# Order of the 512- and 256-column products in the half blocks of a two-layer streaming encoder

## The chip, the cores and the metric

The kernel runs on one core of one Trainium2 chip. The time is the device time of one execution in microseconds (us). The profile is of another execution of the same program; its engines are PE (TensorE matmuls), PEld (TensorE weight loads), DVE (VectorE), ACT (ScalarE), POOL (GpSimd) and SP (which issues most DMAs).

## The reference

Two layers on 256 tokens of width 2048, all float32. Layer 0 is a gated DeltaNet mixer, layer 1 a chunked softmax attention; around the mixers stand four large projections, which are the matrix products spoken of here.

```python
def gated_deltanet(h, w_in, conv_w, a_log, dt_bias, out_norm_w, w_out):
    proj = h @ w_in          # 2048 -> 4*2048 + 32
    qkv = silu(causal_depthwise_conv(proj[..., :3*2048], conv_w))
    ...                      # L2 norms, decay, delta rule in chunks of 64, scan
    return (rms_norm(o, out_norm_w) * silu(z)) @ w_out

def chunk_band_attention(h, w_in, q_norm_w, k_norm_w, rel_bias, w_out):
    proj = h @ w_in          # 2048 -> 4*2048
    ...                      # 9-chunk key band, bias, softmax, gate silu(z)
    return o @ w_out

for i in range(2):
    h = h + mixer[i](rms_norm(h, norm_w[i]))
```

## The kernel before

All weights are read once from memory, 320 pieces of 512 KB called chunks, in the order of a list `plan`. I number them from 0 in that order. `fetch()` runs up to three chunks ahead (`LOOK`): SP loads the chunk into `wt` (4 buffers), ACT rounds it to `whi` (L195, "hi"), and DVE computes the rest `wlo = wt - whi` (L196, "lo"). `whi` and `wlo` have 3 buffers each, so the hi of a chunk can be made when TensorE has used the hi of the chunk three before it, and likewise the lo.

The activations stand in `xb[:, kt, a, :]` as hi (a = 0) and lo (a = 1), 256 tokens each. A product of weights and activations is hi\*hi + hi\*lo + lo\*hi. In a *half* block (152 of the 320 chunks) a chunk has 256 output features and four k-tiles, and `features2` makes the sum with two kinds of product: a **long** one of 512 columns (hi weights on hi and lo activations side by side, L238) and a **short** one of 256 columns (lo weights on the hi activations, L241). There are eight of each in a chunk (two features' halves `s` times four k-tiles `j`). `GROUP = 2` cuts the chunk into two groups of two k-tiles: four long, four short, four long, four short. Each product loads its own 128x128 weights. A half block is four chunks into one PSUM tile `psp` (2 buffers); when it is done, ACT copies one part of it (`ev`, L304) and DVE adds the other (L305), and the tile is free for the block after the next. The other blocks are *wide* (`features`, L228 to L231, all of 256 columns) and *tokens* (L247 to L249, all of 512 columns).

Work that is not a projection (convolutions L497 and L499, norms, the q/k products L556, their scaling L560, squares L568, the copies L606 and transposition L616 of the inversion) stands in background generators; `step()` runs a piece of them after each group. What comes out is then ordered on each engine by a scheduler when the program is built; each engine runs its list strictly in that order. `pre` lets a chunk wait, in the program's text, until its activations have been written.

Of the kernel before, what the change touches and what calls it, by code (L numbers as in the profile page):

```python
# [14 lines left out]
P = 128  # L15
# [3 lines left out]
KT = D // P  # L19
# [4 lines left out]
NWARM = 12  # L24
TIE0 = 4
TIE = 2
GROUP = 2


C_CONV = 0  # L30
# [10 lines left out]
def tile_hybrid_trunk(  # L41
# [12 lines left out]
    act, dve, pool, pe = nc.scalar, nc.vector, nc.gpsimd, nc.tensor  # L54
# [9 lines left out]
    def ps_small():  # L64
        return pss.tile([P, 512], F32, name="pss", tag="pss")
# [19 lines left out]
    ps = ps_small()  # L85
# [124 lines left out]
    def step(n=1):  # L210

        while now:
            now.pop(0)()
        for _ in range(n):
            lanes = (bgq, bg2) if turn[0] else (bg2, bgq)
            turn[0] ^= 1
            for lane in lanes:
                if advance(lane):
                    break
# [10 lines left out]
        pe.matmul(ps, lhsT=hi[:, j, fs], rhs=xb[:, kt, 1, :], start=False, stop=False, skip_group_check=True)  # L230
        pe.matmul(ps, lhsT=lo[:, j, fs], rhs=xb[:, kt, 0, :], start=False, stop=(kt == KT - 1), skip_group_check=True)  # L231

    def features2(ps, hi, lo, js, ks, xb):


        both = [(s, j) for j in js for s in range(2)]
        for s, j in both:
            pe.matmul(ps[:, s], lhsT=hi[:, j, s * P:(s + 1) * P], rhs=xb[:, ks[j], :, :], start=(ks[j] == 0), stop=False,  # L238
                      skip_group_check=True)
        for s, j in both:  # L240
            pe.matmul(ps[:, s, 0, :], lhsT=lo[:, j, s * P:(s + 1) * P], rhs=xb[:, ks[j], 0, :], start=False,  # L241
                      stop=(ks[j] == KT - 1), skip_group_check=True)

    def tokens(ps, t, j, kt, hi, lo, xb):
        ts_ = slice(t * P, (t + 1) * P)
# [7 lines left out]
    def chunk(kind, ps, xb, rate=1, pre=None):  # L253
        i = state["use"]
        state["use"] += 1
        while state["next"] < min(i + 1 + LOOK, len(plan)):
            fetch()
        hi, lo = fetched.pop(i)
        kc = KC * 512 // plan[i][3]
        ks = [plan[i][2] * kc + j for j in range(kc)]  # L260
        f, ns = KINDS[kind]
        if i == len(plan) - 1:

            out_pre(ps)
            for s in range(ns):
                fs = slice(s * P, (s + 1) * P)
                for j, kt in enumerate(ks):
                    for w, a in ((hi, 0), (hi, 1), (lo, 0)):
                        pe.matmul(ps[:, s, 0, :], lhsT=w[:, j, fs], rhs=xb[:, kt, a, :], start=False,
                                  stop=(kt == KT - 1 and w is lo), skip_group_check=True)  # L270
                out_part(s, ps)
            return
        if kind == "half":
            for j in range(0, kc, GROUP):
                js = range(j, j + GROUP)
                if pre is not None:
                    for jj in js:
                        pre(ks[jj])
                features2(ps, hi, lo, js, ks, xb)
                step(rate)  # L280
            return
        for j, kt in enumerate(ks):
            if pre is not None:
                pre(kt)
            for s in range(ns):
                f(ps[:, s], s, j, kt, hi, lo, xb)
            step(rate)
# [6 lines left out]
    def block(kind, xb, rate=1, pre=None):  # L294
        ps = acc(kind)
        for _ in range(CPH if kind == "half" else CPB):
            chunk(kind, ps, xb, rate, pre)
        return ps
# [10 lines left out]
    def pair(xb, rate=1, pre=None):  # L309

        evs = []
        for _ in range(2):
            joined(block("half", xb, rate, pre), evs)
        return evs
# [17 lines left out]
    def split_tiles():  # L332
        return slot("xb", 32, F32R).rearrange("p (k a t) -> p k a t", k=KT, a=2)
# [32 lines left out]
    xb = split_tiles()  # L366
# [460 lines left out]
    for gi in range(4):  # L827
        ps = pair(xb, 2) if gi else block("features", xb, pre=x_split)
# [11 lines left out]
    for gi in range(3):  # L840
        ps = block("tokens", xb, 2 if gi else 1)
# [5 lines left out]
    for gi in range(4):  # L847
        ps = pair(xb)
# [63 lines left out]
    for n in (CUT, CPB - CUT):  # L912
        for j in range(2):
            if n != CUT and j == 0:
                drain()
            for _ in range(n):
                chunk("features", pa[j], gmem["b"], 2, ready(gmem))
            if n != CUT:
                a_done(j, pa[j], 4 * j, 4 * j + 4)
# [20 lines left out]
    xb = hmem["x"]  # L940
    pb, evs = [acc("half") for _ in range(2)], []
    for n in (CUTH, CPH - CUTH):
        for j in range(2):
            if n != CUTH and j == 0:
                drain()
            for _ in range(n):
                chunk("half", pb[j], xb, 2, ready(hmem))
            if n != CUTH:
                joined(pb[j], evs)
# [127 lines left out]
    last = {}  # L1077

    def out_pre(ps):
        last["o"] = o = wk("cv")  # L1080
        dve.tensor_tensor(out=o[:, 0:2, :], in0=ps[:, :, 1, :], in1=h_r[:, 14:16, :], op=ALU.add)

    def out_part(s, ps):
        o = last["o"][:, s, :]
        dve.tensor_tensor(out=o, in0=ps[:, s, 0, :], in1=o, op=ALU.add)
        nc.sync.dma_start(out=ov[:, 14 + s, :], in_=o)
# [69 lines left out]
```

## Time and profile before

| | us |
|---|---|
| median of the runs | 1024.39 |
| the profiled execution | 1024.26 |
| its span (first to last instruction) | 1022.4 |
| PE busy | 1007.9 (99%) |
| PEld busy | 881.1 (86%) |
| DVE busy | 694.8 (68%) |
| ACT busy | 520.2 (51%) |

The span is what the profiler saw between the first and the last instruction; 1.9 us of the execution lie around it. Matmuls overlap in the pipeline, so the time of one is read from the start of one to the start of the next, not from its own duration.

### The profile page before, as it was taken

To read this page: it belongs to the slowest core of one execution; us is meant where nothing else is said; L and a number is where in the kernel's file an instruction comes from. 1 tells how busy PE (TensorE), PEld (TensorE's weight loads), DVE (VectorE), ACT (ScalarE), POOL (GpSimd) and SP (SyncE) were. 2 spreads that over 40 slices of the span, in tenths; PEclk is the share of its full clock that TensorE was granted. 3 is DMA by queue.
4 is the path that set the end of the run, shared out by engine and by line. 5 is a ranking of instruction groups with operands and counts; after the bars stand their busy time and mean duration, and the time that the engine had idled before them with its cause. 6 is when DMAs were issued, how large, how long until landed. Compare 5 with 4: busy or idle time off the path is not lost.

```text
span 1022.4 us, 15569 instructions
## 1 busy us (share of the span) xinstructions
PE 1007.9 (99%) x6094; PEld 881.1 (86%) x6094; DVE 694.8 (68%) x1111; ACT 520.2 (51%) x720; POOL 76.3 (7%) x91
## 2 busy tenths in 40 slices
PE   8999999999999999999999999999999999999998
PEld 7988788888788989899988888888888888889987
DVE  6699879998799587755766555444456666656553
ACT  7465756453646555544654444444445555555442
POOL 1004000112000000001000000000011010101000
PEclk9999999999999999999999999999999999999999
DMA  8655566555576355545856766666665555554572
GB/s 292 177 147 144 162 175 180 143 164 158 157 199 165 105 145 145 158 151 157 255 186 183 228 207 205 190 194 195 188 188 176 148 178 151 167 163 146 174 227 72
DMA packets 133736, 177.55 MB, mean 174 GB/s; under 512 B 7584, under 2 KB 89632, under 8 KB 133664
## 3 DMA queue, kind: packets, MB, share of 16 engines
q1 hardware_dynamic: 132512, 172.38, 57.1%
q0 software_dynamic: 1152, 4.19, 1.2%
q8 instruction: 47, 0.77, 0.3%
q14 instruction: 25, 0.20, 0.1%
HBM read 174.46 MB, written 2.10 MB: 173 GB/s over the span
## 4 chain that ended last, share of the span: by engine, by line
PE 95%; DVE 2%; ACT 1%; DMA 1%; issue 1%; SPq 0%; DVEq 0%; ACTq 0%
PE psp L238 27%; PE psp L241 14%; PE psp L248 11%; PE psp L249 11%; PE psp L247 11%; PE psp L231 4%; PE psp L228 4%; PE psp L230 4%; PE pss L556 2%; PE pss L753 1%; PE pss L992 1%; PE pss L1011 1%; PE pss L1047 1%; DMA wt<-in_a_w_in_dram 1%; DVE wlo L196 1%; PE pss L1037 1%
## 5 line engine op out<-in xcount | busy, mean ns | idle before, releaser
L196 DVE TENSOR_TENSOR wlo<-wt,whi 128x1024 fp32r<-128x1024 f32 (+1 forms) x321 | 392.9, 1226 | 247.2 <-ACT whi L195 238.8
L195 ACT CAST whi<-wt 128x1024 fp32r<-128x1024 f32 (+1 forms) x321 | 336.7, 1050 | 410.9 <-PE psp L238 164.0
L238 PE MATMUL psp<-xb,whi 128*128 128x512 f32 x960 | 265.7, 396 | 3.6 <-DVE ev L305 2.0
L248 PE MATMUL psp<-wlo,xb 128*128 128x512 f32 x512 | 201.1, 393 | 1.6 <-DVE wlo L196 1.6
L249 PE MATMUL psp<-whi,xb 128*128 128x512 f32 x512 | 201.5, 393 | 0.0
L247 PE MATMUL psp<-whi,xb 128*128 128x512 f32 x512 | 200.0, 391 | 0.0
L238 PEld LDWEIGHTS psp<-xb,whi 128*128 128x128 f32 x960 | 165.0, 190 | 25.9 <-DVE ev L305 2.2
L241 PEld LDWEIGHTS psp<-xb,wlo 128*128 128x128 f32 x960 | 148.4, 189 | 20.1
L241 PE MATMUL psp<-xb,wlo 128*128 128x256 f32 x960 | 157.6, 283 | 0.0
L248 PEld LDWEIGHTS psp<-wlo,xb 128*128 128x128 f32 x512 | 96.1, 188 | 21.7 <-DVE wlo L196 2.0
L247 PEld LDWEIGHTS psp<-whi,xb 128*128 128x128 f32 x512 | 96.2, 188 | 20.1 <-ACT whi L195 0.3
L249 PEld LDWEIGHTS psp<-whi,xb 128*128 128x128 f32 x512 | 96.2, 188 | 19.1
L228 PE MATMUL psp<-g,whi 128*128 128x256 f32 x256 | 73.4, 287 | 0.0
L230 PE MATMUL psp<-g,whi 128*128 128x256 f32 x256 | 73.3, 287 | 0.0
L231 PE MATMUL psp<-g,wlo 128*128 128x256 f32 x256 | 72.7, 284 | 0.0
L238 PE MATMUL psp<-g,whi 128*128 128x512 f32 x248 | 67.7, 394 | 0.0
L499 DVE SCALAR_TENSOR_TENSOR cv<-raw,sm,cv 128x254 f32<-128x254 f32 (+2 forms) x144 | 61.8, 474 | 0.1
L230 PEld LDWEIGHTS psp<-g,whi 128*128 128x128 f32 x256 | 49.1, 192 | 0.2
L228 PEld LDWEIGHTS psp<-g,whi 128*128 128x128 f32 x256 | 49.1, 192 | 0.1
L231 PEld LDWEIGHTS psp<-g,wlo 128*128 128x128 f32 x256 | 49.1, 192 | 0.1
L238 PEld LDWEIGHTS psp<-g,whi 128*128 128x128 f32 x248 | 42.4, 189 | 5.7
L241 PEld LDWEIGHTS psp<-g,wlo 128*128 128x128 f32 x248 | 38.1, 189 | 5.3
(239 smaller groups left out, 980.1 us busy)
## 6 DMA issues: line engine op xcount, KB each, us to landing
wt<-in_b_w_in_dram SPq DMA_DIRECT2D x128, 512.0 KB, 3.7
wt<-in_a_w_in_dram SPq DMA_DIRECT2D x127, 512.0 KB, 3.9
wt<-in_a_w_out_dram SPq DMA_DIRECT2D x32, 512.0 KB, 4.5
wt<-in_b_w_out_dram SPq DMA_DIRECT2D x32, 512.0 KB, 4.0
g<-in_xT_dram SPq DMA_DIRECT2D x8, 256.0 KB, 4.5
dl<-in_xT_dram POOLq DMA_DIRECT2D x4, 512.0 KB, 5.4
dl<-in_relb_dram POOLq DMA_DIRECT2D x4, 512.0 KB, 5.2
out_dram<-cv SPq DMA_DIRECT2D x2, 512.0 KB, 4.2
```

The source lines that it names most:

```text
L195: act.copy(out=hi[:, js], in_=wt[:, js])
L196: dve.tensor_tensor(out=lo[:, js], in0=wt[:, js], in1=hi[:, js].bitcast(F32), op=ALU.subtract)
L228: pe.matmul(ps, lhsT=hi[:, j, fs], rhs=xb[:, kt, 0, :], start=(kt == 0 and s % 2 == 0), stop=False, skip_group_check=True)
L230: pe.matmul(ps, lhsT=hi[:, j, fs], rhs=xb[:, kt, 1, :], start=False, stop=False, skip_group_check=True)
L231: pe.matmul(ps, lhsT=lo[:, j, fs], rhs=xb[:, kt, 0, :], start=False, stop=(kt == KT - 1), skip_group_check=True)
L238: pe.matmul(ps[:, s], lhsT=hi[:, j, s * P:(s + 1) * P], rhs=xb[:, ks[j], :, :], start=(ks[j] == 0), stop=False, skip_group_check=True)
L241: pe.matmul(ps[:, s, 0, :], lhsT=lo[:, j, s * P:(s + 1) * P], rhs=xb[:, ks[j], 0, :], start=False, stop=(ks[j] == KT - 1), skip_group_chec ...
L247: pe.matmul(ps, lhsT=xh, rhs=hi[:, j, :], start=(kt == 0), stop=False)
L248: pe.matmul(ps, lhsT=xh, rhs=lo[:, j, :], start=False, stop=False)
L249: pe.matmul(ps, lhsT=xl, rhs=hi[:, j, :], start=False, stop=(kt == KT - 1))
L499: dve.scalar_tensor_tensor(out=cv[:, i, s:], in0=raw[:, i, :T - s], scalar=conv_w(i0 + i, 3 - s), in1=cv[:, i, s:], op0=ALU.mult, op1=ALU.add)
L556: pe.matmul(dst, lhsT=kq[:, a, i, c:c + P], rhs=rhs, start=(n == 0), stop=(n == 2))
```

## The change

The groups are gone. In a half chunk all eight long products now stand together and all eight short ones together, and the order of the two alternates from chunk to chunk: the first and third chunk of a block begin with the long ones, the second and fourth with the short ones. So the short products at the end of one chunk meet the short ones of the next, and runs of sixteen alike come about. Inside a run the k-tiles now follow each other within one feature half (`s` outside, `j` inside; before `j` was outside). `features2` is a generator and yields after each run, so there are still two `step()` calls for a chunk; `pre` is called once, for the chunk's last k-tile. The last chunk of the program has its own code and is as it was.

```diff
--- before.py
+++ after.py
@@ -24,7 +24,6 @@
 NWARM = 12
 TIE0 = 4
 TIE = 2
-GROUP = 2
 
 
 C_CONV = 0
@@ -230,16 +229,22 @@
         pe.matmul(ps, lhsT=hi[:, j, fs], rhs=xb[:, kt, 1, :], start=False, stop=False, skip_group_check=True)
         pe.matmul(ps, lhsT=lo[:, j, fs], rhs=xb[:, kt, 0, :], start=False, stop=(kt == KT - 1), skip_group_check=True)
 
-    def features2(ps, hi, lo, js, ks, xb):
-
-
-        both = [(s, j) for j in js for s in range(2)]
-        for s, j in both:
-            pe.matmul(ps[:, s], lhsT=hi[:, j, s * P:(s + 1) * P], rhs=xb[:, ks[j], :, :], start=(ks[j] == 0), stop=False,
-                      skip_group_check=True)
-        for s, j in both:
-            pe.matmul(ps[:, s, 0, :], lhsT=lo[:, j, s * P:(s + 1) * P], rhs=xb[:, ks[j], 0, :], start=False,
-                      stop=(ks[j] == KT - 1), skip_group_check=True)
+    def features2(ps, hi, lo, ks, xb):
+
+
+        both = [(s, j) for s in range(2) for j in range(len(ks))]
+        turns = (ks[0] // len(ks)) % 2
+        for n, long in enumerate((not turns, turns)):
+            for s, j in both:
+                w = (hi if long else lo)[:, j, s * P:(s + 1) * P]
+                last = n == 1 and ks[j] == KT - 1
+                if long:
+                    pe.matmul(ps[:, s], lhsT=w, rhs=xb[:, ks[j], :, :], start=(ks[j] == 0), stop=last,
+                              skip_group_check=True)
+                else:
+                    pe.matmul(ps[:, s, 0, :], lhsT=w, rhs=xb[:, ks[j], 0, :], start=False, stop=last,
+                              skip_group_check=True)
+            yield
 
     def tokens(ps, t, j, kt, hi, lo, xb):
         ts_ = slice(t * P, (t + 1) * P)
@@ -271,12 +276,9 @@
                 out_part(s, ps)
             return
         if kind == "half":
-            for j in range(0, kc, GROUP):
-                js = range(j, j + GROUP)
-                if pre is not None:
-                    for jj in js:
-                        pre(ks[jj])
-                features2(ps, hi, lo, js, ks, xb)
+            if pre is not None:
+                pre(ks[-1])
+            for _ in features2(ps, hi, lo, ks, xb):
                 step(rate)
             return
         for j, kt in enumerate(ks):
```

The program has the same instructions on every engine as before. In their order, longs that follow each other make 98 runs in place of 314 and shorts 109 in place of 322 (57 runs of sixteen longs, 17 of eight; 55 of sixteen shorts, 14 of eight; the others are broken by background products). The scheduler has also moved background work.

The first place is on PE, chunks 31, 32 and 33 (`whi_1209`, `whi_1234`, `whi_1256` and their lo; `psp_1207` and `psp_1299` are the PSUM tiles of two blocks). Before:

```order
L238 MATMUL psp_1207<-xb_108,whi_1209 128x512 x4
L241 MATMUL psp_1207<-xb_108,wlo_1210 128x256 x4
L238 MATMUL psp_1207<-xb_108,whi_1209 128x512 x4
L241 MATMUL psp_1207<-xb_108,wlo_1210 128x256 x4
L238 MATMUL psp_1299<-xb_108,whi_1234 128x512 x4
L241 MATMUL psp_1299<-xb_108,wlo_1235 128x256 x4
L238 MATMUL psp_1299<-xb_108,whi_1234 128x512 x4
L241 MATMUL psp_1299<-xb_108,wlo_1235 128x256 x4
L238 MATMUL psp_1299<-xb_108,whi_1256 128x512 x4
L241 MATMUL psp_1299<-xb_108,wlo_1257 128x256 x4
L238 MATMUL psp_1299<-xb_108,whi_1256 128x512 x4
L241 MATMUL psp_1299<-xb_108,wlo_1257 128x256 x4
```

and now:

```order
L245 MATMUL psp_1207<-xb_108,wlo_1210 128x256 x8
L242 MATMUL psp_1207<-xb_108,whi_1209 128x512 x8
L242 MATMUL psp_1299<-xb_108,whi_1234 128x512 x8
L245 MATMUL psp_1299<-xb_108,wlo_1235 128x256 x8
L245 MATMUL psp_1299<-xb_108,wlo_1257 128x256 x8
L242 MATMUL psp_1299<-xb_108,whi_1256 128x512 x8
```

Chunk 31 begins with its shorts, its longs meet those of chunk 32, and the shorts of 32 meet those of 33.

The second place is on DVE, at the addition that frees the PSUM tile `psp_1080` for chunk 32 (`ev_1222`, L305 before, L307 now). Before:

```order
L196 TENSOR_TENSOR wlo_1210<-wt_1208,whi_1209 128x1024
L527 TENSOR_REDUCE ssq_113<-raw_952 128x8
L196 TENSOR_TENSOR wlo_1235<-wt_1233,whi_1234 128x1024
L320 TENSOR_TENSOR raw_1098<-ev_1003,rB_561 128x512
L320 TENSOR_TENSOR raw_1098<-ev_1095,rB_561 128x512
L196 TENSOR_TENSOR wlo_1257<-wt_1255,whi_1256 128x1024
L499 SCALAR_TENSOR_TENSOR cv_1101<-raw_1098,sm_76,cv_1101 128x255 x2
L305 TENSOR_TENSOR ev_1222<-psp_1080,ev_1222 128x512
L499 SCALAR_TENSOR_TENSOR cv_1101<-raw_1098,sm_76,cv_1101 128x255
```

and now:

```order
L195 TENSOR_TENSOR wlo_1235<-wt_1233,whi_1234 128x1024
L529 TENSOR_REDUCE ssq_113<-raw_952 128x8
L195 TENSOR_TENSOR wlo_1257<-wt_1255,whi_1256 128x1024
L322 TENSOR_TENSOR raw_1098<-ev_1003,rB_561 128x512
L322 TENSOR_TENSOR raw_1098<-ev_1095,rB_561 128x512
L195 TENSOR_TENSOR wlo_1279<-wt_1277,whi_1278 128x1024
L501 SCALAR_TENSOR_TENSOR cv_1101<-raw_1098,sm_76,cv_1101 128x255 x2
L307 TENSOR_TENSOR ev_1222<-psp_1080,ev_1222 128x512
L501 SCALAR_TENSOR_TENSOR cv_1101<-raw_1098,sm_76,cv_1101 128x255
```

The subtraction for chunk 34 (`wlo_1279`) now stands ahead of that addition; before, it stood behind it.

The third place is on DVE between the subtractions for chunk 50 (`wlo_1769`) and chunk 53 (`wlo_1855`). Before (up to the first rows behind `wlo_1855`):

```order
L196 TENSOR_TENSOR wlo_1769<-wt_1767,whi_1768 128x1024
L305 TENSOR_TENSOR ev_1804<-psp_1636,ev_1804 128x512
L320 TENSOR_TENSOR raw_1807<-ev_1651,rB_561 128x512
L196 TENSOR_TENSOR wlo_1792<-wt_1790,whi_1791 128x1024
L320 TENSOR_TENSOR raw_1807<-ev_1804,rB_561 128x512
L545 TENSOR_TENSOR tt_1608<-cv_1539,tt_1608 128x4x256
L196 TENSOR_TENSOR wlo_1825<-wt_1823,whi_1824 128x1024
L499 SCALAR_TENSOR_TENSOR cv_1810<-raw_1807,sm_76,cv_1810 128x255 x4
L196 TENSOR_TENSOR wlo_1855<-wt_1853,whi_1854 128x1024
L499 SCALAR_TENSOR_TENSOR cv_1810<-raw_1807,sm_76,cv_1810 128x254 x4
```

and now (20 more rows follow, the last of them `wlo_1855`):

```order
L195 TENSOR_TENSOR wlo_1769<-wt_1767,whi_1768 128x1024
L307 TENSOR_TENSOR ev_1804<-psp_1636,ev_1804 128x512
L562 TENSOR_TENSOR dl_112<-pss_1654,dl_112 128x2x256
L562 TENSOR_TENSOR dl_112<-pss_1655,dl_112 128x2x128
L562 TENSOR_TENSOR dl_112<-pss_1672,dl_112 128x2x256
L322 TENSOR_TENSOR raw_1807<-ev_1804,rB_561 128x512
L562 TENSOR_TENSOR dl_112<-pss_1673,dl_112 128x2x128
L570 ISA dg_1682,ssk_114<-dl_112,ident_93 128x128
L570 ISA ssk_114 128x1
L195 TENSOR_TENSOR wlo_1792<-wt_1790,whi_1791 128x1024
L570 ISA dg_1684,ssk_114<-dl_112,ident_93 128x128
L570 ISA ssk_114 128x1
```

The scalings L560 (now L562) and squares L568 (now L570) of the q/k products, which stood behind `wlo_1855`, now stand ahead of it. Counted from `wlo_1521` (chunk 43), there stand before `wlo_1855`, besides the ten subtractions, one L305, eight L499, one L542, eight L560 (four of each size) and six L568 more than before. On PE the products L556 that they read have moved ahead by about three chunks as well. From chunk 144 on, the order on DVE differs by single rows. On SP two weight loads of the last projection stand one row earlier. At the start of the inversion, L606 (ACT) and L616 (DVE) stood ahead of the hi and lo of chunk 77 and now stand ahead of those of chunk 75.

## Rows read from the trace of the kernel before

**Rows 1.** The page: busy time of each engine.

```profile
PE 1007.9 (99%) x6094; PEld 881.1 (86%) x6094; DVE 694.8 (68%) x1111; ACT 520.2 (51%) x720; POOL 76.3 (7%) x91
```

**Rows 2.** Waits of PE: who waited for whom, us in total, times, longest.

```profile
PE psp L238 <- DVE ev L305: 2.0, 1, 2.0
PE psp L248 <- DVE wlo L196: 1.6, 1, 1.6
```

**Rows 3.** Timeline of PE, half block: start, duration, form, count in the row.

```profile
520.37 1.09 PE L238 MATMUL psp<-g,whi 128*128 128x512 f32 x4
521.30 0.63 PE L241 MATMUL psp<-g,wlo 128*128 128x256 f32 x4
...
525.98 0.40 PE L238 MATMUL psp<-g,whi 128*128 128x512 f32 x1
```

**Rows 4.** Timeline of PE, all-256 wide block and all-512 tokens block.

```profile
16.19 0.28 PE L231 MATMUL psp<-xb,wlo 128*128 128x256 f32 x1
...
20.26 0.28 PE L228 MATMUL psp<-xb,whi 128*128 128x256 f32 x1
...
631.87 0.39 PE L249 MATMUL psp<-whi,xb 128*128 128x512 f32 x1
...
639.80 0.39 PE L248 MATMUL psp<-wlo,xb 128*128 128x512 f32 x1
```

**Rows 5.** Timeline of PE: the longer runs of the kernel before.

```profile
128.10 2.02 PE L238 MATMUL psp<-xb,whi 128*128 128x512 f32 x8
129.95 0.63 PE L241 MATMUL psp<-xb,wlo 128*128 128x256 f32 x4
...
151.40 2.00 PE L238 MATMUL psp<-xb,whi 128*128 128x512 f32 x8
153.24 0.64 PE L241 MATMUL psp<-xb,wlo 128*128 128x256 f32 x4
...
155.52 1.12 PE L241 MATMUL psp<-xb,wlo 128*128 128x256 f32 x8
156.47 0.86 PE L238 MATMUL psp<-xb,whi 128*128 128x512 f32 x3
```

**Rows 6.** Timelines around chunk 32's wait; last row: windows, 0.90 is the granted clock.

```profile
118.04 1.71 PE L238 MATMUL psp<-xb,whi 128*128 128x512 f32 x4 [2.02 <-DVE ev L305]
...
122.03 0.63 PE L241 MATMUL psp<-xb,wlo 128*128 128x256 f32 x4
...
117.30 0.68 DVE L305 TENSOR_TENSOR ev<-psp,ev 128x512 f32<-128x512 f32 x1
...
116.98 1.03 ACT L195 CAST whi<-wt 128x1024 fp32r<-128x1024 f32 x1
...
120.00:130.00 10.00, 10.00 (x52) 8.61 (x52) 6.69 (x11) 5.38 (x5) 0.00 (x0) 0.90 0.52 142
```

**Rows 7.** Timelines of DVE and PE, chunks 44 to 53.

```profile
149.40 1.23 DVE L196 TENSOR_TENSOR wlo<-wt,whi 128x1024 fp32r<-128x1024 f32 x1 [0.67 <-ACT whi L195]
152.25 1.23 DVE L196 TENSOR_TENSOR wlo<-wt,whi 128x1024 fp32r<-128x1024 f32 x1 [1.63 <-ACT whi L195]
155.70 1.22 DVE L527 TENSOR_REDUCE ssq<-raw 128x8 f32<-128x1024 f32 x1 [2.22 <-ACT raw L525]
...
175.86 1.21 DVE L196 TENSOR_TENSOR wlo<-wt,whi 128x1024 fp32r<-128x1024 f32 x1
...
182.42 1.09 PE L238 MATMUL psp<-xb,whi 128*128 128x512 f32 x4
```

**Rows 8.** Timeline of DVE: what the background instructions take.

```profile
109.64 1.22 DVE L542 TENSOR_TENSOR kT<-g,kT 128x1024 fp32r<-128x1024 f32 x1
...
161.72 1.65 DVE L499 SCALAR_TENSOR_TENSOR cv<-raw,sm,cv 128x255 f32<-128x255 f32 x4
...
178.77 1.02 DVE L560 TENSOR_TENSOR dl<-pss,dl 128x512 f32<-128x512 f32 x2
...
183.94 0.28 DVE L568 CUSTOM_DVE_ANT_0 dg<-dl,ident 128x128 f32<-128x128 f32 x1
```

## The prediction

> **What bounds the kernel now.** I read the page's busy times first: PE is busy 99% of the span [rows 1], so TensorE sets the end, and a change counts only if it alters the time from one matmul's start to the next or PE's few waits. The list of PE's waits comes next: it is short, and two entries matter, 2.0 us once for a PSUM tile that DVE had not freed (L305) and 1.6 us once for a lo that DVE had not made (L196) [rows 2]. Then the timeline of PE, where the half blocks are one long train. Four long and four short products take (525.98 - 520.37)/4 = 1.4025 us, of which the longs have 521.30 - 520.37 = 0.93 [rows 3].
>
> The same products in unbroken trains are the yardstick. In the tokens block 35 starts lie between 631.87 and 639.80: 0.2266 us for a product of 512 columns. In the first wide block 34 lie between 16.19 and 20.26: 0.1197 us for one of 256 [rows 4]. Four and four would take 0.906 + 0.479 = 1.385 us; they take 1.4025. So one pair of runs, a run of longs and a run of shorts, costs 0.0175 us over the trains. The longs lose 0.024 (0.93 against 0.906) and the shorts win 0.0065: a long product is slow for the first places behind a change of kind, a short one quick.
>
> **Part 1, fewer runs (TensorE alone).** What a longer run loses can be read in the kernel before, where the scheduler happened to put two chunks' longs or shorts together. Eight longs took 129.95 - 128.10 = 1.85 us and 153.24 - 151.40 = 1.84, against 8 x 0.2266 = 1.813: 0.037 and 0.027 lost, 0.032 in the mean. Eight shorts took 156.47 - 155.52 = 0.95 against 0.958: 0.008 won [rows 5]. So the loss belongs to the entry into a run and hardly grows with its length; I take the same 0.032 - 0.008 = 0.024 us for a pair of runs of sixteen, which this trace does not show. Before there are 314 runs of longs and 322 of shorts, some 318 pairs: 318 x 0.0175 = 5.6 us. After, 98 and 109, some 103 pairs: 103 x 0.024 = 2.5 us. **The gain is 3.1 us.** Its bounds: starts are given to 0.01 us, so a pair of long runs may cost 0.014 to 0.038, and the gain is 1.7 to 4.1. Per clean pair of chunks the forecast is 16 x 0.2266 + 0.032 + 16 x 0.1197 - 0.008 = 5.565 us in place of 5.61.
>
> The new order within a run costs nothing in my sum. Longs now go four times into the same PSUM bank with a new moving operand each; in the tokens block three go into one bank in a row, each with another operand, at 0.2266 [rows 4].
>
> The Trainium skill has a rule by which order could not matter at all. Its page "TensorE: Matmul & The Clock Gate", section "Back-to-back issue gap", gives a gap of N/2.4 + 2.5 ns, which is an estimate of 0.216 us for 512 columns and 0.109 for 256, with no term for what ran before. The trace has 0.2266 and 0.1197 and a dependence on the neighbours [rows 3 to 5], so I go by the rows; by the page this part would be worth 0.
>
> **Part 2, the PSUM tile of chunk 32.** Before, PE waited 2.02 us here for the addition L305, which ended at 117.30 + 0.68 = 117.98 [rows 6]. Now the lo of chunk 34 stands ahead of that addition on DVE. It takes 1.23 us [rows 7], and it needs the hi of chunk 34, whose cast before ran from 116.98 to 118.01 [rows 6]. That cast now stands earlier on ACT, but needs chunk 31's longs to be done, which now come last in that chunk. PE was done with chunk 31 at about 116.0 (118.04 less the wait of 2.02), so the cast would run to 117.0, lo 34 to 118.2, two pieces of convolution (0.82, from [rows 8]) to 119.0 and the addition to 119.7: 1.7 later than before. What part 1 has saved by then brings PE and the cast forward alike, so **the wait grows by 1.7 us**; bounds 0 (DVE gets there early) and 2.2 (the saving does not reach the cast). Queued behind the addition on DVE are only convolution pieces and the next lo. After the wait of before, TensorE ran slow: the granted clock was 0.90 over 120 to 130, which is in part the lower of its two levels, 1.2 GHz, and eight longs and four shorts took 122.03 - 118.04 = 3.99 us where 2 x 0.93 + 0.47 = 2.33 is usual, 1.66 us lost [rows 3, 6]. That loss I leave as it is.
>
> **Part 3, lo made late while DVE is full.** In chunks that begin with shorts the lo is needed 0.93 us earlier than before. And between chunks 43 and 53 the background chain has been pulled ahead, so that more of it stands in front of each lo. Up to lo 53 it is eight L499 at 0.41, one L305 at 0.68, one L542 at 1.22, eight L560 at 0.51 and six L568 at 0.28 [rows 6, 8]: 3.3 + 0.7 + 1.2 + 4.1 + 1.7 = 11.0 us. Lo 53 ended at 177.07 and would now end at 188.1, if nothing absorbed that. DVE's own idle time does: 0.67 + 1.63 + 2.22 = 4.5 us in this stretch [rows 7], so 183.6. Chunk 53 began at 182.42 [rows 7]; with part 2's delay of 1.7 less part 1's gain so far (3.1 x 45/151 = 0.9) PE gets there at about 183.2. So with the idle time filled the loss is 0.4; with none of it filled 4.9 us. The products on PE that feed this work have moved ahead too, so most of it should be ready: **I take 1.0 us**, bounds 0 and 4.9. The clock may fall once more after a wait of the size of part 2's: another 1.7, in the upper bound alone.
>
> **The rest.** At the entry to the inversion the transposition now stands two chunks earlier in the lists, behind products that are also two chunks earlier. The wait of 1.6 us for a lo is there [rows 2]; it may go (-1.6) or grow by as much, and I take 0. From chunk 144 on the order on DVE differs by single instructions and PE's list of waits has nothing of that stretch; the earlier `pre`, the two swapped loads on SP and the earlier or later release of hi and lo are covered there by that slack, and cost what a late lo costs if it is gone. The end of the program is unchanged.
>
> **Sum.** -3.1 + 1.7 + 1.0 + 0 = -0.4 us on the profiled 1024.26, that is 1023.9. The median of the runs shown is 0.1 higher, so I say **1024.0 us**: no change that a measurement can tell.
>
> **Rivals.**
> First, the gain comes whole. DVE's idle time takes in all the work that was pulled ahead, part 3 costs nothing, part 2's wait stays as it is and the inversion's wait goes: 1024.4 - 3.1 - 1.6 = 1019.7; with the latter wait left, 1021.3. For it: PE's background products moved with DVE's list. Against it: the addition that frees the PSUM tile visibly stands behind one more lo.
> Second, and slower than before: the late lo. From the point where less than about 3 us of DVE's 4.5 us can be filled (then the loss is over 2 us and with part 2 outweighs the gain), because pieces of the chain wait on ACT or on PE as L527 did for 2.22 us [rows 7], PE stands at the shorts that begin chunk 53 or one of its neighbours for up to 4.9 us, the clock falls once more (1.7), and part 2 has its 2.2: 1024.4 - 3.1 + 2.2 + 4.9 + 1.7 = 1030.1.
> Third, order costs nothing inside TensorE: the slow places would go with background products or chunk borders that fell there, not with the change of kind. Then part 1 is 0 and parts 2 and 3 remain: 1024.4 + 2.7 = 1027.1. It is the case that the page's gap rule stands for. Against it: the loss is in the clean stretch, where nothing else runs on PE [rows 3].
> That the change does not do what it says is excluded by the order: 314 runs become 98.
>
> **How the numbers follow.** Forecast 0.50; gain whole 0.20; late lo 0.17; order without effect 0.10; something not thought of 0.03. The range takes in the first three at most of their width: 1019.5 to 1030.5. A measurement of this kernel can tell about 2%, 20 us, from no change. None of the cases reaches that on either side; from the last 0.03 I give 0.01 to faster, 0.02 to slower, and 0.97 to within 2%.
>
> **What would show it.** Right: in the timeline of the changed kernel a clean pair of chunks takes 5.56 to 5.58 us, a run of sixteen longs 3.65 to 3.66, and PE's list of waits has one of 3 to 4 us for L305 near 118. Part 3 is wrong if no wait of PE for a lo stands between 140 and 200, or if they sum to over 3 us. Part 1 is wrong if the clean pair still takes 5.61, or if runs of sixteen do not settle at 0.2266. What would make the whole wrong by more than the range is a wait in a stretch that has none now, above all behind 330 us, where the lists hardly differ, or more than one fall of the clock.

## The result and the profile after

The changed kernel takes 1025.38 us (median of 20 runs) beside 1022.93 of the kernel before (20 runs): a ratio of 1.0028, 95% interval 1.0018 to 1.0037. It is slower by some 2.9 us, small but clear, where the forecast was a change of -0.4. Two runs of the kernel before, at 1239.97 and 2028.42 us, are slow ones and stand outside the ratio. The profiled execution is 1027.16 us with a span of 1025.3.

The page after, busy time of each engine, which answers to [rows 1]:

```profile
PE 1007.6 (98%) x6094; PEld 883.8 (86%) x6094; DVE 694.4 (68%) x1111; ACT 520.5 (51%) x720; POOL 74.3 (7%) x91
```

PE's busy time is what it was (1007.6 for 1007.9), and the span is 2.9 us longer: the gain inside TensorE and a slower clock cancel in the busy time, and the rest is waiting. PE's list of waits, which answers to [rows 2] (total us, times, longest):

```profile
PE psp L242 <- DVE ev L307: 4.4, 2, 4.2
PE pss L668 <- issue: 1.7, 1, 1.7
PE psp L242 <- DVE raw L325: 1.7, 1, 1.7
PE psp L253 <- DVE wlo L195: 1.6, 1, 1.6
```

The wait for chunk 32's PSUM tile (L305 before, L307 now) is 4.2 us for 2.0. The second row was 0.6 before, in a row that neither [rows 2] nor the prediction has:

```profile
PE pss L666 <- issue: 0.6, 1, 0.6
```

"Issue" is time in which PE waited for nothing that the profile shows. The third row was 1.6 before, the fourth is the inversion's lo, as before.

A clean pair of chunks in the timeline of PE, which answers to [rows 3] (start, duration, form, count):

```profile
519.38 3.82 PE L242 MATMUL psp<-g,whi 128*128 128x512 f32 x16
523.03 2.08 PE L245 MATMUL psp<-g,wlo 128*128 128x256 f32 x16
524.95 1.32 PE L242 MATMUL psp<-g,whi 128*128 128x512 f32 x5
```

Sixteen longs take 523.03 - 519.38 = 3.65 us and the pair 524.95 - 519.38 = 5.57, against 5.61 before. For this pair the gain inside TensorE is there, and of the size forecast.

Around chunk 32, timelines of PE, ACT and DVE, which answer to [rows 6]:

```profile
113.45 2.00 PE L242 MATMUL psp<-xb,whi 128*128 128x512 f32 x8
119.67 3.78 PE L242 MATMUL psp<-xb,whi 128*128 128x512 f32 x8 [4.21 <-DVE ev L307]
123.25 2.84 PE L245 MATMUL psp<-xb,wlo 128*128 128x256 f32 x16
...
115.49 1.04 ACT L194 CAST whi<-wt 128x1024 fp32r<-128x1024 f32 x1 [1.05 <-PE psp L242]
...
117.01 1.21 DVE L195 TENSOR_TENSOR wlo<-wt,whi 128x1024 fp32r<-128x1024 f32 x1
118.14 0.87 DVE L501 SCALAR_TENSOR_TENSOR cv<-raw,sm,cv 128x255 f32<-128x255 f32 x2
118.93 0.68 DVE L307 TENSOR_TENSOR ev<-psp,ev 128x512 f32<-128x512 f32 x1
```

PE is done with chunk 31 at 119.67 - 4.21 = 115.46 and stands until the addition ends at 119.61. Ahead of it on DVE are the lo of chunk 34 and two pieces of convolution. Then the eight longs take 123.25 - 119.67 = 3.58 us where 1.84 is usual: they run at the lower level of the clock.

Windows with PE's busy time and, after the counts, the granted clock:

```profile
110.00:120.00 10.00, 5.79 (x33) 0.91 0.61 165
120.00:130.00 10.00, 10.00 (x46) 0.75 0.32 99
...
320.00:330.00 10.00, 8.28 (x214) 0.83 0.56 162
```

0.75 over ten microseconds is five at the lower level, 1.2 GHz, and five at 2.4; with the 0.91 ahead of it (1.8 us) the clock was low for 6.8 us, from 118.2 to 125.0. It fell 1.5 us before the wait ended; that part cost nothing, so that the low clock lost (6.8 - 1.5)/2 = 2.7 us. Before, it was 0.90 in the second window and low for 3.4 us in all (118.5 to 121.9), all of it behind the wait: 1.7 us lost. The third window has a fall that is new, 326.4 to 329.8. Just ahead of it stands the wait called issue, in the second burst of 32x32 products of the inversion:

```profile
324.51 0.19 PE L668 MATMUL pss<-g 32*32 32x32 f32 x1
326.43 0.27 PE L668 MATMUL pss<-g 32*32 32x32 f32 x2 [1.72 <-issue]
...
327.00 0.80 PE L242 MATMUL psp<-xb,whi 128*128 128x512 f32 x1
```

The kernel before has this burst at 329.95 to 332.81 and its clock whole there (PE, PEld, DVE, ACT, POOL, clock):

```profile
330.00:340.00 10.00, 9.45 (x275) 8.78 (x274) 5.91 (x10) 6.15 (x9) 0.00 (x0) 1.00 0.37 105
```

**The ledger.** Starts of the same chunks in the two profiled executions, from the timelines of PE:

```
chunk        31      32      40      80     144     192   end of span
before   113.05  118.04  142.98  273.76  495.11  630.71  1022.37
after    112.49  119.67  145.35  275.52  498.93  634.02  1025.33
later     -0.56   +1.63   +2.37   +1.77   +3.82   +3.31    +2.95
```

Up to chunk 31 the order gains (0.3 of the 0.56 lie ahead of chunk 8, where nothing is changed). Between 31 and 40 2.9 us are lost (wait and clock), between 80 and 144 2.05 (the second burst and the clock behind it), and in the other stretches it gains again: 0.6, 0.5 and 0.36.

### The profile page after: what moved, and what is told of

The parts are those of the page before. It is cut to its first block, busy times and chain, and to the rows that moved or that the text cites. A ratio compares the mean times of both kernels' runs of the same rounds, so it can differ in the third digit from the quotient of the medians.

```text
span 1025.3 us, 15595 instructions
## 1 busy us (share of the span) xinstructions
PE 1007.6 (98%) x6094; PEld 883.8 (86%) x6094; DVE 694.4 (68%) x1111; ACT 520.5 (51%) x720; POOL 74.3 (7%) x91
## 4 chain that ended last, share of the span: by engine, by line
PE 96%; DVE 1%; ACT 1%; issue 1%; DMA 1%; SPq 0%; ACTq 0%
PE psp L242 27%; PE psp L245 14%; PE psp L253 11%; PE psp L254 11%; PE psp L252 11%; PE psp L230 4%; PE psp L227 4%; PE psp L229 4%; PE pss L558 2%; PE pss L755 1%; PE pss L994 1%; PE pss L1013 1%; PE pss L1049 1%; DMA wt<-in_a_w_in_dram 1%; DVE wlo L195 1%
## 5 line engine op out<-in xcount | busy, mean ns | idle before, releaser
L242 PE MATMUL psp<-xb,whi 128*128 128x512 f32 x960 | 237.0, 395 | 6.1 <-DVE ev L307 4.4
L242 PEld LDWEIGHTS psp<-xb,whi 128*128 128x128 f32 x960 | 177.0, 190 | 40.9 <-DVE ev L307 5.3
L245 PE MATMUL psp<-xb,wlo 128*128 128x256 f32 x960 | 132.5, 286 | 0.0
L245 PEld LDWEIGHTS psp<-xb,wlo 128*128 128x128 f32 x960 | 126.4, 193 | 5.3
L242 PE MATMUL psp<-g,whi 128*128 128x512 f32 x248 | 59.4, 391 | 0.0
L242 PEld LDWEIGHTS psp<-g,whi 128*128 128x128 f32 x248 | 45.5, 188 | 8.7
L229 PEld LDWEIGHTS psp<-g,whi 128*128 128x128 f32 x256 | 49.1, 192 | 0.2
L227 PEld LDWEIGHTS psp<-g,whi 128*128 128x128 f32 x256 | 49.1, 192 | 0.1
L230 PEld LDWEIGHTS psp<-g,wlo 128*128 128x128 f32 x256 | 49.1, 192 | 0.1
L245 PEld LDWEIGHTS psp<-g,wlo 128*128 128x128 f32 x248 | 31.9, 191 | 1.2
```

Of the source, the lines that this page charges most:

```text
L227: pe.matmul(ps, lhsT=hi[:, j, fs], rhs=xb[:, kt, 0, :], start=(kt == 0 and s % 2 == 0), stop=False, skip_group_check=True)
L242: pe.matmul(ps[:, s], lhsT=w, rhs=xb[:, ks[j], :, :], start=(ks[j] == 0), stop=last, skip_group_check=True)
L245: pe.matmul(ps[:, s, 0, :], lhsT=w, rhs=xb[:, ks[j], 0, :], start=False, stop=last, skip_group_check=True)
```

## Experiments

Theories. **Mine**: the order gains inside TensorE what was forecast, and three things give it back: the longer wait at chunk 32, more time at the low clock behind waits, and the wait called issue. **Rival A**: alternation is what costs, since chunks with the shorts in front want their lo early. **Rival B**: the order within a run costs (four products in a row into one half of the PSUM tile). All kernels below were run beside the kernel before; ratios are to it.

### 1. Without alternation

```diff
-        turns = (ks[0] // len(ks)) % 2
+        turns = 0
```

> Every half chunk begins with its eight long products; no alternation. My theory (TensorE gains, waits and the clock give it back): a chunk has one pair of runs instead of two, so the gain inside TensorE is 152 x (2 x 0.0175 - 0.024) = 1.7 us against the kernel before, half of the changed kernel's 3.1, and a clean pair of chunks takes 5.58 to 5.59 us. On DVE the addition that frees chunk 32's PSUM tile has two lo fewer ahead of it than in the changed kernel, one fewer than before, so the wait near 118 shrinks to 0.8 us or less and the granted clock there stays at its upper level: another 1.2 + 1.7 us. Together 3 to 5 us faster than before, ratio 0.995 to 0.997. Rival (the alternation itself costs, because shorts in front want their lo early): also faster than the changed kernel, but with the wait near 118 as in the kernel before, so only 1.7 us faster than it, ratio 0.998. Rival (the order inside TensorE gives nothing): the clean pair stays at 5.61.

Measured: ratio 0.9968 (0.9956 to 0.998), 1018.62 us for 1022.25. A clean pair takes 517.60 - 512.01 = 5.59 us. Timelines of PE and DVE of this kernel, and its wait list:

```profile
512.01 2.00 PE L242 MATMUL psp<-g,whi 128*128 128x512 f32 x8
...
517.60 1.78 PE L242 MATMUL psp<-g,whi 128*128 128x512 f32 x7
...
114.36 1.12 PE L245 MATMUL psp<-xb,wlo 128*128 128x256 f32 x8
115.32 2.00 PE L242 MATMUL psp<-xb,whi 128*128 128x512 f32 x8
...
112.70 0.68 DVE L307 TENSOR_TENSOR ev<-psp,ev 128x512 f32<-128x512 f32 x1
```

```profile
PE pss L473 <- ACT dl L478: 2.2, 1, 2.2
PE psp L242 <- DVE ev L307: 1.9, 1, 1.9
```

Chunk 32 starts at 115.32 without a wait, and the granted clock was 1.00 in all windows from 100 to 140 and from 300 to 350. The two waits in the list are elsewhere, at 85 to 87 and at 47.7 to 49.55. The first is new and helps to explain why chunk 32 no longer waits: PE is 2.2 us later there, and the addition is not; it ends at 113.38, 1.9 us before PE needs it. So the wait moved more than it went: from the start of chunk 8 to that of chunk 32 it is 115.32 - 31.36 = 83.96 us here and 118.04 - 33.94 = 84.10 before. What went is the fall of the clock, and the gain inside TensorE is left. In the runs of either kernel in which the clock never fell, the spans are 1016.1 to 1016.5 us here and 1017.7 to 1018.1 before: 1.6 us, the 1.7 forecast for TensorE. The rest of the 3.6 us is a clock that falls less often or where it costs less (mean granted clock of the runs 0.9979 here, 0.9971 before). Against rival A this run does not yet decide.

### 2. The new order from chunk 144 on

```diff
+            if i < 144:
+                for j in range(0, kc, 2):
+                    ...
+                    features2_old(ps, hi, lo, js, ks, xb)
+                    step(rate)
+                return
```

> The new order only from chunk 144 on, the old groups of two k-tiles before it. My theory: up to chunk 143 every engine's list is the old one, so the wait of 2.0 us near 118 and its one short low stretch of the clock are as before and no second low stretch is added; what is left is the gain inside TensorE, 63 of 152 chunks or 31 pairs x 0.045 = 1.4 us, ratio 0.9986 (0.9982 to 0.9994). Rival (alternation costs wherever it stands): no gain or a loss, ratio 1.000 or more.

Measured: 0.9983 (0.9969 to 0.9996), 1020.77 us. Two rows of the timeline of PE:

```profile
518.19 3.82 PE L251 MATMUL psp<-g,whi 128*128 128x512 f32 x16
...
523.75 2.46 PE L251 MATMUL psp<-g,whi 128*128 128x512 f32 x10
```

The pair is 5.56 us, and the ratio holds the amount worked out (0.9986), but in part by luck. From the start of chunk 144 to the end the profiles take 527.26 us before, 526.39 here and 526.46 in experiment 1: 0.87 us gained where 1.4 was worked out, and 0.80 of it without alternation. (A block that background products break, chunks 164 to 167, takes 12.48 us here, 12.11 before and 12.09 in experiment 1.) The rest of the ratio's 1.7 us goes with the clock of the runs, 0.9978 against 0.9971. From chunk 144 on alternation costs nothing, and rival A falls there. Ahead of chunk 144 the wait list of the changed kernel speaks against it: the only wait for a lo above 0.8 us is the inversion's, as long as before. What alternation does there, it does by moving other work, the addition for chunk 32 and the burst.

### 3. The new order from chunk 36 on

The same edit with `if i < 36`.

> The new order from chunk 36 on, the old groups for chunks 8 to 35, so that DVE's list at the addition for chunk 32's PSUM tile is the old one. My theory: the wait near 118 is 2.0 us and the low stretch of the clock after it 3.4 us, as before; the gain inside TensorE is 3.1 x 124 / 152 = 2.5 us; the two bursts of 32x32 products of the inversion still follow three longs, so the wait of 1.7 us there and the low stretch behind it (1.1 + 1.7 us) probably stay: 0.3 us slower than before, ratio 1.0003, or 0.9976 if they go. Rival (the loss lies in late lo behind chunk 36, not in chunk 32's wait): as slow as the changed kernel, ratio 1.003.

Measured: 0.9999 (0.9982 to 1.0016), 1021.32 us; no verdict between the two forecasts of my theory, but not 1.003. In the profile the wait at chunk 32 is 2.0 us again and, unlike what I expected, the wait called issue is gone. Yet its 12 runs have a mean granted clock of 0.9952, as low as the changed kernel's 0.9953: five of them stand at 0.993 or below, with spans of 1022.3 to 1024.2 us against 1017.5 to 1018.2 where the clock was 0.998. Why the clock falls more often in this kernel than in the kernel before is open. In the profiled run it fell at 50.5 and at 333.8, the second time behind a wait of only 0.5 us.

### 4. The wait at chunk 32 filled

```diff
+            if i == 31:
+                for _ in range(16):
+                    pe.matmul(ps[:16, 0], lhsT=zero_r, rhs=xb[:, 0, :, :], start=False, stop=True, skip_group_check=True)
```

> The changed kernel with sixteen more products of 512 columns on zero weights (16 columns wide, one more small activation on ACT makes them) behind chunk 31, into its own PSUM tile: 16 x 0.2266 = 3.6 us of work that adds zero, inside the wait of 4.2 us. My theory (the clock is the larger part of the loss): chunk 32 starts when it did, near 119.7, the clock stays at its upper level through 118 to 130, and the run is 3.4 us faster than the changed kernel (6.8 us at half speed): ratio to the kernel before 0.9995. The background products of the inversion fall elsewhere in this order, so the new low stretch at 326 may go as well: another 2.8 us, ratio 0.997. Rival (the loss is the wait itself, or late work on DVE): no gain over the changed kernel, ratio 1.003 or more.

Measured: 1.0041 (1.0028 to 1.0054), 1026.62 us: slower than the changed kernel, against both forecasts of my theory. The windows of PE and the head of its wait list show why:

```profile
120.00:130.00 10.00, 10.00 (x65) 1.00 0.37 108
320.00:330.00 10.00, 6.37 (x210) 0.74 0.53 152
```

```profile
PE pss L673 <- issue: 3.6, 1, 3.6
```

At chunk 32 the fill did what it should: the clock is 1.00 where it was 0.75. But background work moved, and the wait called issue in the second burst grew from 1.7 to 3.6 us, with a low clock from 324.8, inside that wait, to 331.6. What I had taken for a side matter was a cause of its own.

### What the wait called issue is

The page's list of DMA queues in the changed kernel has this row (packets, MB, share of the DMA engines):

```profile
q8 instruction: 47, 0.77, 0.3%
```

Forty-seven packets of 16384 bytes, one for about every 260 of TensorE's 12,226 records (products and weight loads, numbered by their starts). Set beside the second burst, from the trace's records of packets and products (us, from start to start, so that a stop is 0.2 us longer than in the wait list):

```
kernel           burst begins   packet landed   PE stopped   resumed   at record
no alternation         323.41          322.33   (no stop)
before                 329.95          330.69       331.25    331.99        4033
changed                322.65          324.99       324.51    326.43        4033
zero products          321.57          325.51       323.19    327.01        4034
```

In three kernels PE stops at the same place in its list and goes on 1.3 to 1.5 us after such a packet has landed, wherever the burst itself began. (The profiles of new144 and jout below have it too, at record 4033: 0.25 and 1.86 us, 1.4 us after a packet.) That is what it would look like if PE had run out of instructions. In the trains of ordinary products a packet's worth of records takes 13 to 30 us and nothing is noticed; the 192 products of the burst take 2.3 us where nothing stops them. What decides when a packet is asked for is not in the trace; but the later it lands after the burst's begin (-1.1, 0.7, 2.3 and 3.9 us in the four rows), the longer the stop (0, 0.74, 1.92 and 3.82). The Trainium skill, page "Runtime: NRT & Kernel Launch", section "Instruction fetch mechanics", says that instructions come in 16 KiB blocks of 256 and that crossing a block's edge is mostly hidden. The traces agree on the size; in this burst the crossing is not hidden.

### 5 and 6. The list moved against the packets' edges

If that is so, the wait must go, or come, when TensorE's list is moved by some instructions and nothing else changes. The warm-up products at the start, whose results nobody uses, can be cut into more and shorter ones; the order of all engines behind them stays the same.

```diff
-NWARM = 12
+NWARM = 92
...
-        pe.matmul(ps, lhsT=warm[:, :P], rhs=warm, start=True, stop=True)
+        pe.matmul(ps[:, :66], lhsT=warm[:, :P], rhs=warm[:, :66], start=True, stop=True)
```

> The changed kernel with the twelve warm-up products of 512 columns at the start cut into ninety-two of 66 columns: about the same work there, and the same order on every engine behind it, but everything on TensorE stands 160 instructions later in its list. The traces show 47 packets of 16384 bytes in the queue named instruction, and the wait called issue near 324 ended behind such a packet, at the same place in TensorE's list (record 4033) in the kernel before, the changed one and the one with zero products. My theory (the wait is for instructions, and it is long where the place at which a packet is asked for stands inside the second burst of 32x32 products): the wait of 1.7 us near 324 goes, and with it the low stretch of the clock behind it: 1.9 + 1.7 = 3.6 us faster than the changed kernel, ratio to the kernel before 0.9995 (0.9985 to 1.001). Rival (the wait belongs to the bursts themselves, to what they read or to the weights that load for them): it stays, ratio 1.003.

Measured: 1.0005 (0.9996 to 1.0014), 1022.22 us beside 1021.97. The wait in the burst is gone. A short one is left behind the burst, at the next edge: PE stops at 326.43 and goes on at 327.00, at record 4290, 1.5 us after a packet landed at 325.51.

```profile
PE pss L683 <- issue: 0.4, 1, 0.4
```

The wait at chunk 32 is still 4.2 us, with its low clock (0.85 and 0.81 in the windows 110 to 130). In the window of the burst the clock is whole:

```profile
320.00:330.00 10.00, 9.65 (x272) 1.00 0.42 114
```

The counter-test puts an edge into the burst of the kernel without alternation, with a hundred warm-up products of 61 columns.

> The counter-test: the kernel without alternation, which has no wait called issue, with its warm-up cut into a hundred products of 61 columns, so that all of TensorE's list stands 176 instructions later and a packet's edge falls about 40 products into the second burst of 32x32 products, as it does in the changed kernel. All engines keep their order. My theory (instructions): a wait of 1.5 to 3.8 us appears in that burst near 325 and mostly a low stretch of the clock behind it, 2 to 5 us slower than without the shift, ratio to the kernel before 0.999 to 1.002. Rival (the bursts' own): no such wait, ratio 0.997 as without the shift.

Measured: 1.0011 (1.0001 to 1.002), 1023.36 us. The wait list's head and two windows:

```profile
PE pss L668 <- issue: 2.2, 1, 2.2
```

```profile
320.00:330.00 10.00, 7.81 (x334) 1.00 0.50 133
330.00:340.00 10.00, 10.00 (x111) 0.83 0.27 82
```

The wait has appeared, at record 4290, 257 behind the place of the other kernels and the same as in experiment 5, and PE goes on at 329.80, 1.4 us after a packet landed at 328.41. The clock falls behind it (331.1 to 334.5). From 0.9968 to 1.0011: 4.4 us for moving a list by 176 instructions. Not all of it need be the burst's: this profile also has low stretches at 51.2 and 259.4, behind waits of 1.9 and 1.6 us that the kernel without the shift has as well, without a fall in its profile. The stage by itself, from the start of chunk 80 to that of chunk 144, took 223.4 us in the changed kernel and 220.6 with its list moved, 220.7 without alternation and 224.6 with that list moved. The same places in the list, the same delay behind the packet, and the wait taken away and brought about at will: that it is a wait for instructions is shown.

### 7. The order within a run

```diff
-        both = [(s, j) for s in range(2) for j in range(len(ks))]
+        both = [(s, j) for j in range(len(ks)) for s in range(2)]
```

> The changed kernel with the k-tile outside and the feature half inside again: the long and short products of a run go to the two halves of the PSUM tile in turn, as before, and each weight tile order is the old one; runs and alternation stay. My theory: the order within a run costs nothing, so a clean pair of chunks takes 5.56 to 5.57 us and the ratio to the kernel before is that of the changed kernel, 1.003. Rival (four products in a row into one half of the tile are what costs): a shorter clean pair and 1 us or more faster than the changed kernel, ratio 1.002 or less.

Measured: 1.0029 (1.0018 to 1.0041), and 524.53 - 518.96 = 5.57 us for the pair:

```profile
518.96 3.82 PE L242 MATMUL psp<-g,whi 128*128 128x512 f32 x16
...
524.53 2.68 PE L242 MATMUL psp<-g,whi 128*128 128x512 f32 x11
```

Rival B falls; the waits and the falls of the clock near 118 and 326 are those of the changed kernel, too.

### 8. Both remedies

The zero products of experiment 4 together with fifty warm-up products of 122 columns.

> The changed kernel with both remedies: the sixteen products on zero weights that fill the wait at chunk 32, and the warm-up cut into fifty products of 122 columns, so that TensorE's list stands 76 instructions later and a packet's edge falls behind, not into, the first products of the second burst. My theory: the wait for instructions goes (3.6 us in the profile of the kernel with zero products alone) and the clock stays at its upper level at 118 to 130 and at 325 to 332; what is left of the loss is chunk 32's wait of 2.2 us, against 3.1 us of gain inside TensorE and the 1.7 us of clock that the kernel before loses at 118: 2 to 3 us faster than the kernel before, ratio 0.9975 (0.996 to 0.999), and some 3 us faster than the changed kernel with the shift alone (1.0005). Rival (the filled wait gives nothing, because the clock is not what the wait costs): the ratio of the shift alone, 1.0005, or more.

Measured: 0.9989 (0.9977 to 1.0001), 1020.61 us beside 1022.5. Timeline and windows of PE:

```profile
113.35 3.86 PE L286 MATMUL psp<-xb,zero_r 128*16 128x512 f32 x16
117.75 2.12 PE L243 MATMUL psp<-xb,whi 128*128 128x512 f32 x8 [0.54 <-DVE ev L311]
...
120.00:130.00 10.00, 10.00 (x64) 1.00 0.37 106
320.00:330.00 10.00, 10.00 (x259) 1.00 0.52 152
```

PE starts chunk 32 no earlier, 0.54 us after the zero products, but at the full clock, and no wait for instructions is left. Against the shift alone that is 0.0016, 1.6 us, where I expected 3; the two intervals just overlap. In the profiles chunks 32 to 40 take 23.30 us here and 26.09 with the shift alone, so the profiled run with the shift lost more there than the mean run does. Over the runs the granted clock rose from 0.9972 to 0.9987, which is worth 1.5 us of 1019, so the gain goes with the clock.

### 9. Eight and eight, alternating from chunk 144 on

```diff
-        turns = (ks[0] // len(ks)) % 2
+        turns = (ks[0] // len(ks)) % 2 if state["use"] > 144 else 0
```

> Eight long and eight short products in every half chunk up to 143 without alternation, alternation from chunk 144 on, where the engines' lists have slack. My theory: the kernel without alternation plus what alternation adds inside TensorE on 63 chunks, 31 pairs x 0.0225 = 0.7 us: ratio to the kernel before 0.996 (0.995 to 0.997), the fastest of all so far by a little. Rival (alternation costs wherever it stands): slower than the kernel without it, ratio 0.997 or more.

Measured: 0.9958 (0.9944 to 0.9972), 1018.11 us beside 1021.97: the lowest ratio of all, from five runs, and faster than both kernels of the study. Its interval overlaps that of experiment 1 (0.9956 to 0.998), and the profiles speak against the 0.7 us worked out: from chunk 144 on this kernel takes 526.41 us and that of experiment 1 526.46. So the ratio agrees with the forecast by luck.

## Why the prediction was wrong

**Part 1 was right in the clean pair and too high in the whole.** The clean pair was forecast at 5.565 us and takes 5.57; sixteen longs 3.65 to 3.66, measured 3.65; new144, mixed and jout repeat it. The whole was less than the 3.1 us of the sum: in the ledger the stretches without a long wait give some 0.3, 0.6, 0.5 and 0.36, and 16 pairs of chunks between 80 and 144 would add 0.7 by the pair's 0.043: 2.5 us. The 24 pairs between 144 and 192 would give 1.0 by that and gave 0.5, because chunks 164 to 171, where background products break the runs and PE waits once for 0.2 us, take 0.4 more than before. The third rival (order without effect) is refuted. The formula that the prediction set against the rows, from the Trainium skill, page "TensorE: Matmul & The Clock Gate", section "Back-to-back issue gap", is given there for an isolated product, not for a stream in which each product loads its weights; so it does not say that order could not matter here.

**Part 2 was right in place and in its upper bound.** I took 1.7 us, bounds 0 and 2.2; the wait grew from 2.02 to 4.21. The addition ended at 119.61, forecast 119.7. It was PE that came earlier than I had it, at 115.46 for 116.0: 0.3 us of that lie ahead of chunk 8, the rest is what part 1 had saved. The cast of hi 34 came earlier too (115.49), but DVE then ran two other pieces before lo 34, so the saving did not reach the addition.

**The steps that failed** are two terms that the sum has at nothing. The larger is **"The rest"**, of which I said "I take 0". For the inversion it prices the lo alone, and that wait stayed at 1.6. What cost stands in the inversion too, but in the second burst, which the list of waits before had with 0.6 us behind the word issue and which I did not ask about. There PE's stop grew from 0.74 to 1.92 us, and the clock fell behind it for 3.4 us, where it had been whole: 1.2 + 1.7 = 2.9 us in the profile. Over the runs it is 2.3 of the 2.9 us by which the changed kernel is slower: with its list moved (experiment 5) the ratio is 1.0005 in place of 1.0028, and the kernel of experiment 7, run beside it with the list unmoved, has 1.0029. Experiments 5 and 6 also show that it has nothing to do with the order of products as such: the change moved the burst against the edges of TensorE's instruction packets.

The smaller is the sentence behind part 2, on the clock after that wait: **"That loss I leave as it is"**. It did not stay. In the profiles the low stretch went from 3.4 to 6.8 us; 1.5 us of it lie inside the wait, so 2.7 us were lost for 1.7 before, 1.0 more. Filling the wait without shortening it (experiment 8) brings the clock back and gives 1.6 us beside the shift alone. I had put one more fall into the upper bound of part 3 and into the second rival alone, tied to late lo, while the wait that I myself forecast to be twice as long was the likelier cause. Both places together show in the runs: the mean granted clock went from 0.9971 (35 runs of the kernel before beside experiments 1 to 4) to 0.9953, which on 1023 us is at most 1.9 us more lost.

**Part 3 was too high**: 1.0 us with bounds 0 and 4.9, and PE has no wait for a lo between 140 and 200. DVE's idle time between lo 43 and lo 53 did shrink, from 4.5 to 1.3 us, as the first rival had it, and lo 53 ended at 184.82, where I had 183.6 with the idle time filled:

```profile
183.60 1.22 DVE L195 TENSOR_TENSOR wlo<-wt,whi 128x1024 fp32r<-128x1024 f32 x1
...
185.69 2.08 PE L245 MATMUL psp<-xb,wlo 128*128 128x256 f32 x16
```

But PE came later than I had it. The second eight of these shorts are chunk 53's and begin at 186.65, where I had 183.2; the lo had been ready for 1.8 us. I knew that the q/k products had moved ahead and gave PE no time for them: between chunks 40 and 53 it now runs twelve more products L558 (L556 before), six of 512 and six of 256 columns, about 2.1 us by the trains of [rows 4]. The second rival's mechanism did not occur, nor did the time gain of the first, which needed the wait at chunk 32 to stay as it was.

The sum as it came out in the profiles: -0.3 (ahead of chunk 8) - 2.5 (order) + 2.2 (wait at chunk 32) + 1.0 (clock there) + 1.2 (instructions) + 1.7 (clock there) = +3.3. The span grew by 2.95, so the parts are shown, and their sum to some 0.3 us.

## What to carry to other kernels

When TensorE sets the time, a wait costs its length and then whatever the clock does behind it (0, 1.7 and 2.7 us at chunk 32 in the profiles of new144, before and after); price both wherever a change makes a wait longer, and fill what can't be shortened with products that add zero. (That alone made this kernel slower, 1.0041, because it moved the burst.) A small reordering also moves bursts of very short instructions against the edges of the instruction packets, and such a wait ("issue") can be moved away by shifting the list, here by 76 or 160 instructions at its start; look at that before one blames the reordering. And eight and eight without alternation, which was forecast to have half of the gain, was worth more here than the whole; from chunk 144 on it has 0.80 of 0.87 us.

## What was not expected of the hardware

- A wait for instructions on TensorE: 0.6, 1.7, 2.2 and 3.6 us in bursts of 192 products of 32x32 that otherwise take 2.3 us. PE goes on 1.3 to 1.5 us after a packet of 16384 bytes lands.
- Nearly all the spread between the runs of these two kernels goes with the granted clock. The changed kernel's spans are 1025.0 to 1025.5 us at a clock of 0.993, 1023.5 to 1023.9 at 0.995, 1022.1 to 1023.0 at 0.997 and 1021.0 to 1021.4 at 0.998; the kernel before (beside experiments 1 to 4) has 1022 to 1022.9 at 0.995 and 1017.7 to 1018.1 at 1.000. In the profiles the low stretches were 3.4 or 6.8 us long, and most began behind or inside a wait of PE of 1.6 to 4.2 us; a wait of 2.0 at the same place was followed by one in the kernel before and by none in the profile of new144. What decides between the two is open.
- Products on a weight tile of 16 columns take as long as on one of 128: sixteen in 117.75 - 0.54 - 113.35 = 3.86 us, until the last is done, beside the row of 3.82 us for sixteen longs.
